# Gate products by row halves, interleaved score products and a wide head norm in a two-layer hybrid trunk

## The chip, the cores and the metric

The kernel runs on one core of a Trainium2 chip. The metric is the device time of one execution in microseconds; where a kernel was timed several times, the median stands. The trace is that of one profiled execution, whose own time is given beside its span. TensorE (PE in the rows) multiplies matrices, PEld is its loading of weights, VectorE is DVE, ScalarE is ACT, GpSimd is POOL, and SyncE (SP) issues the transfers of weights.

## What is computed

Two layers of a decoder trunk on 512 tokens with 1024 features, in float32. In each layer the RMS-normalised input goes through one wide projection; its columns feed three groups of token mixers, whose outputs, side by side, go through an output projection onto the residual. A convolutional feed-forward net follows. The parts that the change touches:

```python
def head_rmsnorm(o, w):
    y = o * rsqrt(mean(o * o, axis=-1) + NORM_EPS)        # per head of 64
    return y.reshape(B, S, H * d) * w

def rglru_group(xr, gr, ...):                             # 512 features in 8 blocks of 64
    xc = causal_dwconv(xr, conv_w, conv_b)
    r = sigmoid(block products of xc with wa + ba)        # 8 blocks, each 64 x 64
    i = sigmoid(block products of xc with wx + bx)
    log_a = -8 * r * softplus(-lam)
    u = sqrt(-expm1(2 * log_a)) * (i * xc)
    h = scan(h = exp(log_a) * h + u)
    return h * gelu(gr)

def retention_group(q, k, v, g, norm_w):                  # 4 heads of 64, chunks of 128
    per chunk: scores = (q k^T) * decay; o = scores v + (q state) * q_dec; state = ...
    return head_rmsnorm(o, norm_w) * silu(g)

x = x + concat(y_lru, y_ret, y_hg) @ w_out                # the output projection
```

The third mixer (HGRN2, 4 heads of 64) has a head norm of the same form.

## The kernel before

Features lie on the 128 partitions and the 512 tokens along the free axis, so a [128, 512] tile is two heads or two blocks of 64. Every large product takes both operands as two float32r parts (a rounded one, `h`, and the rest, `l`) and three matmuls of 512 columns: h·h, l·h and h·l (`mm3`, lines 320 to 322). The weights arrive as raw float32; for each weight tile ACT makes the rounded part (`wh`) and DVE the rest (`wl`), two tiles ahead of their use. In rows, `pps` is the input projection and the FFN's up projection, `vps` the values, `ops` the output projection, `dps` the FFN's down projection. The small products of the mixers go through `small` (line 326); most take plain float32 operands.

The order of every engine's instructions is written by a program, `Flow`. It emits the stream of large products, and keeps a rough clock of each engine; the mixers are chains (Python generators) whose next step is emitted when that clock says that the step before should be done. Engines then run their own instructions strictly in the emitted order, and wait for each other by data. So an instruction that is late holds up everything behind it on its engine, whatever it belongs to.

In a layer the chains run beside the input projection: first HGRN2 (`hg_...`), then retention in two pairs of heads (`rt_...`, `ft` = 0 and 1), and the RG-LRU (`lr_...`, four tiles `j`), first its four gate tiles, then in a batch twelve exponentials and hyperbolic tangents, four square roots and four scans. The batch waits for the head norms of HGRN2. Only one head norm of the wide kind (`head_norm`, `rsqrt_wide`) may run at a time (`hns`). At the end each of the eight mixed tiles is multiplied by its gate and split into `xh` and `xl` (`split_y`); a tile's place is free only when the last product of the input projection has read the old contents. The output projection reads the eight in the order `YORDER`: two of HGRN2, then the two retention pairs, then four of the RG-LRU. Its first two output tiles each take the first six inputs, then both take the last two.

What the change touches, before:

- RG-LRU gates: `lw` holds the blocks of both weights as block-diagonal 128 x 128 matrices. Per `j` there are two plain float32 products of 128 rows and 512 columns (`lr_ps`), one for each gate, and one sigmoid on 128 partitions for each.
- Retention scores: for each head four products of 64 rows with 128 x 128 results (`rt_ps`), the two heads of a pair one after the other, each with its own wait for a bank.
- Retention's head norm (`head_norm_cols`): squares, four narrow products that put token sums in columns (`hn_ps<-csm,sq`), an inverse root by bit trick and three Newton steps in a dozen small DVE operations (`hc_...`), and eight products that spread the result over the features again (`hn_rps`).
- `head_norm`, until now only HGRN2's: squares, their two float32r parts, two products with a matrix of means (`hn_ps<-hn_h`, `hn_ps<-hn_l`), then Ln, Exp and Square on ACT and three wide operations on DVE.

Of the kernel before, what the change touches and what calls it, by code (L numbers as in the profile page):

```python
# [7 lines left out]
F32 = mybir.dt.float32  # L8
# [33 lines left out]
# columns of the packed float constants  # L42
# [15 lines left out]
# W_in tiles in the order of use: (kind, column, contraction half)  # L58
# [10 lines left out]
# order in which the mixed features enter the output projection  # L69
# [84 lines left out]
class Timed:  # L154
    """An engine whose instructions are counted on the flow's clock."""
# [49 lines left out]
def kernel(ctx, tc, x_in, win, wout, wup, wdn, lruw, params, consts, out):  # L205
    nc = tc.nc

    const = ctx.enter_context(tc.tile_pool(name="const", bufs=1))
# [128 lines left out]
    def rsqrt_cols(pool, ps, shape, name, bufs=1):  # L337
        # seed from the exponent bits, then three Newton steps to full float32
        v = pool.tile(shape, F32, name=f"{name}_v", bufs=bufs)
        r = pool.tile(shape, F32, name=f"{name}_rc", bufs=bufs)  # L340
        t = pool.tile(shape, F32, name=f"{name}_nt", bufs=bufs)
        V.tensor_scalar(out=v, in0=ps, scalar1=EPS, scalar2=None, op0=ALU.add)
        V.tensor_scalar(out=r.bitcast(I32), in0=v.bitcast(I32), scalar1=1, scalar2=None,
                        op0=ALU.logical_shift_right)
        V.tensor_scalar(out=r.bitcast(I32), in0=r.bitcast(I32), scalar1=-1, scalar2=0x5F3759DF,
                        op0=ALU.mult, op1=ALU.add)
        for _ in range(3):
            V.tensor_tensor(out=t, in0=r, in1=r, op=ALU.mult)
# [65 lines left out]
    def finish_norm(n):  # L414
        if n.wide:
            # rb is -2 times the rstd
# [77 lines left out]
    def matmul_tiles(n, count, done, first=False, freed=None):  # L494
        """count weight tiles against the normed input; the first two of a phase leave its last parts for later."""
# [26 lines left out]
    def mixers(l, n):  # L522
# [31 lines left out]
        def head_norm(src, on, key):  # L554
            yield from hns.take()
            sq = mp.tile([128, S], F32, name="lr_a", bufs=4)
            v = mp.tile([128, S], F32, name="lr_a", bufs=4)
# [8 lines left out]
            drop(hns)  # L566
            on[key] = src
# [98 lines left out]
        # -- HGRN2 --  # L666
# [114 lines left out]
        # -- RG-LRU --  # L781
        lw = mp.tile([128, 2, 4, 128], F32, name="lw")
        nc.sync.dma_start(out=lw, in_=lruw[l])

        xc2, xcs, hst = {}, {}, {}

        def lru_conv(j):
# [13 lines left out]
            xcs[j] = xc  # L801
            evt.add(("xc", j))

        def lru_batch():
            js = range(4)
            gts, av = {}, {}
            for j in js:
                yield has(("xc", j))
                pss = []
                for w in range(2):  # L810
                    pss.append((yield from psum([128, S], "lr_ps")))
                for w in range(2):
                    small(0.857, out=pss[w], lhsT=lw[:, w, j, :], rhs=xcs[j])
                yield None
                gts[j] = []
                for w, bn in ((0, "lba"), (1, "lbx")):
                    g = mp.tile([128, S], F32, name=f"lr_g{w}", bufs=4)
                    A.activation(out=g, in_=pss[w], func=AF.Sigmoid, bias=pc(l, bn, j))
                    drop(sm)
                    gts[j].append(g)  # L820
# [41 lines left out]
        # -- retention --  # L862
# [24 lines left out]
        def ret_chain(ft):  # L887
# [6 lines left out]
            st = mp.tile([128, 2, NC, 128], F32, name="st", bufs=2)  # L894
            for h in range(2):
                hd = 2 * ft + h
                hs = slice(64 * h, 64 * h + 64)
                ps = yield from psum([128, NC, 128], "rt_ps")
                for c in range(NC):
                    cs = slice(c * 128, (c + 1) * 128)  # L900
                    small(0.11, out=ps[:, c, :], lhsT=rk[hs, cs], rhs=rq[hs, cs])
                yield None
                V.scalar_tensor_tensor(out=st[:, h], in0=ps, scalar=kin[:, hd:hd + 1],
# [20 lines left out]
            yield from head_norm_cols(o, ron, ("r", ft))  # L924
# [5 lines left out]
        for j in range(4):  # L930
            fl.spawn(lru_conv(j))
            fl.spawn(lru_gate(j))
        fl.spawn(lru_batch())
# [48 lines left out]
        # output projection, added to the residual  # L982
# [39 lines left out]
    def ffn(l, n, nxt):  # L1022
# [69 lines left out]
        def down_and_norm(gi):  # L1092
            # last group by halves of the tokens: the final norm of one half runs beside the other
# [103 lines left out]
    def main():  # L1197
        # the table of the activations is loaded while the first transfers run
# [4 lines left out]
        # the first tiles: input, first weights and constants in the order of need  # L1203
# [68 lines left out]
def _layout(inputs):  # L1272
# [34 lines left out]
    lruw = np.zeros((DEPTH, 128, 2, 4, 128), a["lru_wa"].dtype)  # L1307
    for i, nm in enumerate(("lru_wa", "lru_wx")):
        for b in range(8):
            o = 64 * (b % 2)  # L1310
            lruw[:, o:o + 64, i, b // 2, o:o + 64] = a[nm][:, b]
    ps = []
    for l in range(DEPTH):
        ps += [
            cols(a["norm1_w"][l]), cols(a["norm2_w"][l]), cols(a["lru_conv_w"][l].reshape(-1)),
            cols(a["lru_conv_b"][l]), cols(a["lru_ba"][l]), cols(a["lru_bx"][l]), cols(a["lru_lambda"][l]),
# [65 lines left out]
```

## Time and profile before

| | |
|---|---|
| median of 3 runs | 1201.98 us (1201.81 to 1202.22) |
| span of the profiled execution | 1199.86 us; about 2.1 us of the time lie around the span |
| TensorE | 1176.6 us busy, 98% of the span |
| VectorE, ScalarE, GpSimd | 812.2, 512.6 and 100.7 us busy |
| chain that ended last | TensorE 92% of the span, VectorE 5% |
| mean granted clock of TensorE | 0.995 of full speed |

A matmul's duration in the rows overlaps its neighbours, so the distance between the starts of two products is what one costs the stream. Plain float32 products leave two records each (k_o, rt_ps, lr_ps, hn_ps<-csm and hg_pl), the transposes and the float32r products one; an `x8` is then four products. In the pieces of the chain the duration is the time until the next instruction goes on.

### The profile page before, as it was taken

To read this page: it belongs to the slowest core of one execution; us is meant where nothing else is said; L and a number is where in the kernel's file an instruction comes from. 1 tells how busy PE (TensorE), PEld (TensorE's weight loads), DVE (VectorE), ACT (ScalarE), POOL (GpSimd) and SP (SyncE) were. 2 spreads that over 40 slices of the span, in tenths; PEclk is the share of its full clock that TensorE was granted. 3 is DMA by queue.
4 is the path that set the end of the run, shared out by engine and by line. 5 is a ranking of instruction groups with operands and counts; after the bars stand their busy time and mean duration, and the time that the engine had idled before them with its cause. 6 is when DMAs were issued, how large, how long until landed. Compare 5 with 4: busy or idle time off the path is not lost.

```text
span 1199.9 us, 15340 instructions
## 1 busy us (share of the span) xinstructions
PE 1176.6 (98%) x6044; PEld 967.0 (81%) x6044; DVE 812.2 (68%) x1218; ACT 512.6 (43%) x689; POOL 100.7 (8%) x85
## 2 busy tenths in 40 slices
PE   7989989999999999999999999999999999999996
PEld 6877778888888888888887877788888888888886
DVE  6797878558675467375579775865876746655746
ACT  5414684454443244142441445644544423423423
POOL 0131240000000000000223211400000000000001
PEclk9999999999999999999999999999999999999998
DMA  7222213232323332322341221222223232233221
GB/s 252 86 72 63 78 54 106 88 105 89 104 81 95 108 99 79 119 83 76 108 138 62 63 88 54 87 106 94 100 88 106 67 116 100 88 103 104 79 80 75
DMA packets 36312, 112.29 MB, mean 94 GB/s; under 512 B 4496, under 2 KB 4752, under 8 KB 36240
## 3 DMA queue, kind: packets, MB, share of 16 engines
q1 hardware_dynamic: 34704, 109.22, 28.4%
q10 hardware_dynamic: 1536, 2.10, 0.7%
q8 instruction: 47, 0.77, 0.3%
q14 instruction: 25, 0.20, 0.1%
HBM read 107.10 MB, written 2.10 MB: 91 GB/s over the span
## 4 chain that ended last, share of the span: by engine, by line
PE 92%; DVE 5%; issue 1%; DMA 0%; POOL 0%; SPq 0%; ACT 0%; POOLq 0%; DVEq 0%; ACTq 0%
PE pps L320 19%; PE pps L322 19%; PE pps L321 19%; PE dps L322 7%; PE dps L320 7%; PE dps L321 7%; PE ops L322 2%; PE ops L320 2%; PE ops L321 2%; DVE qp L181 1%; DVE st L181 1%; PE k_o L326 1%; PE lr_ps L326 1%; PE vps L320 1%; PE vps L322 1%
## 5 line engine op out<-in xcount | busy, mean ns | idle before, releaser
L320 PE MATMUL pps<-xh,wh 128*128 128x512 f32 x1024 | 410.1, 400 | 6.8 <-ACT wh L181 5.5
L322 PE MATMUL pps<-xh,wl 128*128 128x512 f32 x1024 | 401.8, 392 | 0.5 <-DVE wl L181 0.5
L321 PE MATMUL pps<-xl,wh 128*128 128x512 f32 x1024 | 401.7, 392 | 0.0
L181 ACT ACTIVATE wh<-raw 128x1024 fp32r<-128x1024 f32 (+2 forms) x210 | 204.4, 976 | 156.1 <-PE dps L321 103.3
L181 DVE TENSOR_TENSOR wl<-raw,wh 128x1024 fp32r<-128x1024 f32 (+2 forms) x210 | 242.1, 1156 | 18.9 <-ACT wh L181 18.8
L320 PEld LDWEIGHTS pps<-xh,wh 128*128 128x128 f32 x1024 | 193.4, 189 | 51.7 <-ACT wh L181 5.5
L322 PEld LDWEIGHTS pps<-xh,wl 128*128 128x128 f32 x1024 | 193.3, 189 | 42.9 <-DVE wl L181 1.2
L321 PEld LDWEIGHTS pps<-xl,wh 128*128 128x128 f32 x1024 | 193.6, 189 | 41.4 <-issue 1.7
L181 DVE SCALAR_TENSOR_TENSOR hs<-pps,rb 128x512 f32<-128x512 f32 x88 | 60.4, 690 | 128.8 <-PE pps L322 128.7
L322 PE MATMUL dps<-gh,wl 128*128 128x512 f32 x320 | 124.5, 389 | 0.0
L320 PE MATMUL dps<-gh,wh 128*128 128x512 f32 x320 | 124.5, 389 | 0.0
L321 PE MATMUL dps<-gl,wh 128*128 128x512 f32 x320 | 124.5, 389 | 0.0
L181 DVE TENSOR_TENSOR x<-x,dps 128x512 f32<-128x512 f32 (+1 forms) x72 | 45.1, 627 | 107.3 <-PE dps L322 106.8
L181 ACT ACTIVATE cg<-hs,prm 128x512 f32<-128x512 f32 x44 | 36.0, 817 | 81.2 <-DVE hs L181 76.6
L320 PEld LDWEIGHTS dps<-gh,wh 128*128 128x128 f32 x320 | 60.1, 188 | 12.5
L321 PEld LDWEIGHTS dps<-gl,wh 128*128 128x128 f32 x320 | 60.1, 188 | 12.5
L322 PEld LDWEIGHTS dps<-gh,wl 128*128 128x128 f32 x320 | 60.1, 188 | 12.4
L181 DVE SCALAR_TENSOR_TENSOR cvv<-hs,prm,cvv 128x511 f32<-128x511 f32 x88 | 65.8, 748 | 1.8
L181 DVE SCALAR_TENSOR_TENSOR cg<-hs,prm,cg 128x511 f32<-128x511 f32 x88 | 65.7, 747 | 1.5
L181 ACT ACTIVATE cg<-cg 128x512 f32<-128x512 f32 x44 | 27.8, 632 | 87.2 <-DVE cg L181 87.1
L181 ACT ACTIVATE gh<-cvv 128x512 fp32r<-128x512 f32 x44 | 27.7, 631 | 76.6 <-DVE cvv L181 76.6
L320 PE MATMUL ops<-xh,wh 128*128 128x512 f32 x128 | 50.5, 395 | 0.0
(207 smaller groups left out, 1330.8 us busy)
## 6 DMA issues: line engine op xcount, KB each, us to landing
raw<-in_wup_dram SPq DMA_DIRECT2D x88, 512.0 KB, 3.5
raw<-in_win_dram SPq DMA_DIRECT2D x46, 512.0 KB, 3.5
raw<-in_wdn_dram SPq DMA_DIRECT2D x48, 384.0 KB, 3.0
raw<-in_wout_dram SPq DMA_DIRECT2D x16, 512.0 KB, 3.6
raw<-in_wdn_dram SPq DMA_DIRECT2D x16, 256.0 KB, 2.6
x<-in_x_dram SPq DMA_DIRECT2D x8, 256.0 KB, 5.5
sw<-ev ACTq DMA_DIRECT2D x32, 64.0 KB, 2.1
out_dram<-hs SPq DMA_DIRECT2D x7, 256.0 KB, 2.0
```

The lines of the kernel that those rows point to most:

```text
L181: return fn(*args, **kw)
L320: T.matmul(out=ps, lhsT=ah, rhs=bh, start=start, stop=False)
L321: T.matmul(out=ps, lhsT=ah, rhs=bl, start=False, stop=False)
L322: T.matmul(out=ps, lhsT=al, rhs=bh, start=False, stop=stop)
L326: T.matmul(**kw)
```

## The change

- RG-LRU gates: `lw` is packed anew: the 64 rows of a block carry its columns for both gates side by side. ACT and DVE split it into `lwh` and `lwl` once a layer, and each convolved tile into `xch` and `xcl`. Per `j` there are six float32r products of 64 rows, 128 results and 512 columns, in turn on the upper and the lower half of the rows, into two banks; then four sigmoids on 64 partitions.
- Retention scores: both banks are taken first, and the eight products of a pair alternate between the heads, that is between the row halves.
- Retention's head norm: `head_norm` with `late=True`, in turn with HGRN2's on the one slot; `head_norm_cols` is not called any more.
- A pool `low` holds the new tiles; `dynamic_dma_scratch_size=1024` is set when the program is built. Lines of comment are gone.

```diff
-        def head_norm(src, on, key):
+        def head_norm(src, on, key, late=False):
             yield from hns.take()
-            sq = mp.tile([128, S], F32, name="lr_a", bufs=4)
-            v = mp.tile([128, S], F32, name="lr_a", bufs=4)
+            if late:
+                yield from sqs.take()
+                sq = mp.tile([128, S], F32, name="sq", bufs=2)
+                v = low.tile([128, S], F32, name="rn_v")
+            else:
+                sq = mp.tile([128, S], F32, name="lr_a", bufs=4)
+                v = mp.tile([128, S], F32, name="lr_a", bufs=4)
...
+        def lru_weights():
+            yield has(("hg_done", 0))
+            A.activation(out=lwh, in_=lw, func=AF.Copy)
+            yield None
+            V.tensor_tensor(out=lwl, in0=lw, in1=lwh.bitcast(F32), op=ALU.subtract)
...
+            h = low.tile([128, S], F32R, name="xch", bufs=2)
+            lo = low.tile([128, S], F32R, name="xcl", bufs=2)
+            A.activation(out=h, in_=xc, func=AF.Copy)
+            yield None
+            V.tensor_tensor(out=lo, in0=xc, in1=h.bitcast(F32), op=ALU.subtract)
...
-                for w in range(2):
-                    small(0.857, out=pss[w], lhsT=lw[:, w, j, :], rhs=xcs[j])
+                h, lo = xcp[j]
+                for p, (w, v) in enumerate(((lwh, h), (lwh, lo), (lwl, h))):
+                    for b in range(2):
+                        bs = slice(64 * b, 64 * b + 64)
+                        small(0.12, out=pss[b], lhsT=w[bs, j, :], rhs=v[bs, :], start=p == 0, stop=p == 2)
                 yield None
-                gts[j] = []
-                for w, bn in ((0, "lba"), (1, "lbx")):
-                    g = mp.tile([128, S], F32, name=f"lr_g{w}", bufs=4)
-                    A.activation(out=g, in_=pss[w], func=AF.Sigmoid, bias=pc(l, bn, j))
+                gts[j] = [mp.tile([128, S], F32, name=f"lr_g{w}", bufs=4) for w in range(2)]
+                for b in range(2):
+                    for w, bn in ((0, "lba"), (1, "lbx")):
+                        to = slice(64 * b, 64 * b + 64)
+                        at = slice(64 * (b ^ w), 64 * (b ^ w) + 64)
+                        A.activation(out=gts[j][w][to, :], in_=pss[b][at, :], func=AF.Sigmoid,
+                                     bias=pc(l, bn, j)[at, :])
...
+            pss = []
+            for h in range(2):
+                pss.append((yield from psum([128, NC, 128], "rt_ps")))
+            for c in range(NC):
+                cs = slice(c * 128, (c + 1) * 128)
+                for h in range(2):
+                    hs = slice(64 * h, 64 * h + 64)
+                    small(0.12, out=pss[h][:, c, :], lhsT=rk[hs, cs], rhs=rq[hs, cs])
...
-            yield from head_norm_cols(o, ron, ("r", ft))
+            yield from head_norm(o, ron, ("r", ft), late=True)
```

Since the order is made by the planner's clock, it moves in many places. Three of them follow. First TensorE in layer 0, at the first output tile (`ops`). Before, the products of the first and the second retention pair (`xh_1838`, then `xh_1846`) stand side by side:

```order
L320 MATMUL ops<-xh_1838,wh 128x512
L321 MATMUL ops<-xl_1839,wh 128x512
L322 MATMUL ops<-xh_1838,wl 128x512
L320 MATMUL ops<-xh_1846,wh 128x512
L321 MATMUL ops<-xl_1847,wh 128x512
L322 MATMUL ops<-xh_1846,wl 128x512
```

After, `xh_1898` is the first retention pair and `xh_1919` the second; the sums of squares for the second pair's norm stand between them:

```order
L321 MATMUL ops<-xh_1898,wh 128x512
L322 MATMUL ops<-xl_1899,wh 128x512
L323 MATMUL ops<-xh_1898,wl 128x512
L327 MATMUL hn_ps<-hn_h,hmean 128x512
L327 MATMUL hn_ps<-hn_l,hmean 128x512
L321 MATMUL ops<-xh_1919,wh 128x512
L322 MATMUL ops<-xl_1920,wh 128x512
L323 MATMUL ops<-xh_1919,wl 128x512
```

The last head norm has moved from some 90 products ahead of the output projection into it.

Second, ACT in layer 0 behind the twelve exponentials of the RG-LRU batch. Before (`qp` are the four square roots, `sq<-ev` sigmoids of gates, `ev<-ev` the GeLU):

```order
L181 ACTIVATE wh<-raw 128x1024 x2
L181 ACT_TABLE_LOAD
L181 ACTIVATE qp<-qp 128x512 x4
L181 ACT_TABLE_LOAD
L181 ACTIVATE sq<-ev 128x512 x2
L181 ACTIVATE wh<-raw 128x1024
L181 ACT_TABLE_LOAD
L181 ACTIVATE ev<-ev 128x512
L181 ACTIVATE wh<-raw 128x1024
```

After, with the Ln and the Exp of the first retention pair's norm (`rn_v`):

```order
L181 ACT_TABLE_LOAD
L181 ACTIVATE rn_v<-hn_ps,eps 128x512
L181 ACTIVATE wh<-raw 128x1024 x2
L181 ACT_TABLE_LOAD
L181 ACTIVATE qp<-qp 128x512 x4
L181 ACT_TABLE_LOAD
L181 ACTIVATE sq<-ev 128x512
L181 ACT_TABLE_LOAD
L181 ACTIVATE rn_v<-rn_v 128x512
L181 ACT_TABLE_LOAD
L181 ACTIVATE ev<-ev 128x512 x2
```

The norm's steps stand between those of the batch, each with a table of its own.

Third, DVE in layer 1 ahead of the output projection. Before (`lr_g<-lr_a,qp` is a scan, `rt_on` a retention pair, `xl` the last part of a mixed tile):

```order
L181 TENSOR_TENSOR ev<-pps,rb 128x512
L181 TENSOR_TENSOR wl<-raw,wh 128x1024
L181 TENSOR_TENSOR xl_6356<-hg_on,xh_6355 128x512
L181 TENSOR_TENSOR xl_6362<-hg_on,xh_6361 128x512
L181 TENSOR_TENSOR xl_6372<-rt_on,xh_6371 128x512
L181 TENSOR_TENSOR lr_g_6033<-lr_g_6033,ev 128x512
L181 TENSOR_TENSOR xl_6379<-rt_on,xh_6378 128x512
```

After:

```order
L181 TENSOR_TENSOR xl_6370<-hg_on,xh_6369 128x512
L181 TENSOR_TENSOR xl_6377<-hg_on,xh_6376 128x512
L181 SCALAR_TENSOR_TENSOR rt_on<-rt_on,prm,ev 128x512
L181 TENSOR_TENSOR xl_6387<-rt_on,xh_6386 128x512
L181 TENSOR_TENSOR lr_g_6137<-lr_g_6137,ev 128x512
L181 TENSOR_TENSOR wl<-raw,wh 128x1024 x2
L181 TENSOR_TENSOR xl_6424<-lr_g_5918,xh_6423 128x512
L181 TENSOR_TENSOR xl_6431<-lr_g_6021,xh_6430 128x512
L181 TENSOR_TENSOR lr_g_6159<-lr_g_6159,ev 128x512
L181 TENSOR_TENSOR xl_6452<-rt_on,xh_6451 128x512
```

The second retention pair's `xl` has moved from two places behind the first pair's to seven places behind it, with its multiplication by the gate just ahead of the first pair's `xl`.

## Rows read from the trace of the kernel before

**Rows 1.** The page: span, and TensorE's busy time with its share and instructions.
```profile
span 1199.9 us, 15340 instructions
PE 1176.6 (98%) x6044; PEld 967.0 (81%) x6044; DVE 812.2 (68%) x1218; ACT 512.6 (43%) x689; POOL 100.7 (8%) x85
```

**Rows 2.** Waits of TensorE: line, waited for, us in total, times, longest.
```profile
PE hn_rps L326 <- DVE hc_rc L181: 3.2, 1, 3.2
```

**Rows 3.** A stretch after that wait: length, busy time by engine, granted clock 0.51, DMA.
```profile
180.30:183.60 3.30, 3.30 (x12) 2.52 (x9) 3.30 (x5) 1.58 (x2) 0.00 (x0) 0.51 0.52 158
```

**Rows 4.** Chain that ended last, small products: start, us until the next, instruction.
```profile
82.84 0.61 PE hg_pl L326 x16
...
97.55 1.08 PE rt_ps L326 x8
...
109.62 3.65 PE k_o L326 x56
...
118.36 0.79 PE hn_ps L326 x8
122.03 1.72 PE lr_ps L326 x4
125.83 1.02 PE hn_rps L326 x16
...
135.73 0.47 PE hn_ps L326 x2
...
153.75 0.50 PE k_mps L326 x12
...
156.54 1.83 PE k_o L326 x28
...
688.53 1.83 PE k_o L326 x28
```

**Rows 5.** Timeline of TensorE in layer 0: start, duration, instruction, count.
```profile
95.66 0.87 PE L326 MATMUL k_o<-qp,k_sv 64*64 64x128 f32 x12
96.46 1.09 PE L326 MATMUL hg_pl<-qp,k 128*64 128x128 f32 x8
```

**Rows 6.** Timeline of TensorE, output projection of layers 0 and 1, first and fourth input.
```profile
197.36 0.40 PE L320 MATMUL ops<-xh,wh 128*128 128x512 f32 x1
...
199.46 0.39 PE L320 MATMUL ops<-xh,wh 128*128 128x512 f32 x1
...
783.65 0.39 PE L320 MATMUL ops<-xh,wh 128*128 128x512 f32 x1
```

**Rows 7.** Timeline of ACT in layer 0: table load, exponentials, weights, four square roots.
```profile
152.45 1.28 ACT L181 ACT_TABLE_LOAD   x1
153.74 0.72 ACT L181 ACTIVATE lr_a<-lr_g,lamc 128x512 f32<-128x512 f32 x1
...
161.69 1.04 ACT L181 ACTIVATE wh<-raw 128x1024 fp32r<-128x1024 f32 x1
...
168.41 2.19 ACT L181 ACTIVATE qp<-qp 128x512 f32<-128x512 f32 x4
```

**Rows 8.** ACT's gate sigmoids, both layers: busy, mean ns of one, idle before.
```profile
L181 ACT ACTIVATE lr_g<-lr_ps,prm 128x512 f32<-128x512 f32 x16 | 10.8, 687 | 16.3 <-PE lr_ps L326 16.3
```

**Rows 9.** Timeline of DVE in layer 1: scan, weights, and 512-column operations.
```profile
774.12 1.21 DVE L181 TENSOR_TENSOR_SCAN lr_g<-lr_a,qp 128x512 f32<-128x512 f32 x1
775.26 1.19 DVE L181 TENSOR_TENSOR wl<-raw,wh 128x1024 fp32r<-128x1024 f32 x1
...
777.04 0.68 DVE L181 TENSOR_TENSOR lr_g<-lr_g,ev 128x512 f32<-128x512 f32 x1
777.64 0.68 DVE L181 TENSOR_TENSOR ev<-pps,rb 128x512 f32<-128x512 f32 x1
```

**Rows 10.** Timeline of POOL in layer 1: the four products ahead of the scans.
```profile
758.96 7.91 POOL L181 TENSOR_TENSOR qp<-qp,lr_g 128x512 f32<-128x512 f32 x4 [1.09 <-ACT qp L181]
```

More of the change, by code (lines that the diff above doesn't have):

```diff
@@ L206 @@
     nc = tc.nc
+    low = ctx.enter_context(tc.tile_pool(name="low", bufs=1, reuse_waits="tile"))
     const = ctx.enter_context(tc.tile_pool(name="const", bufs=1))
@@ L566, in head_norm @@
             drop(hns)
+            if late:
+                drop(sqs)
             on[key] = src
@@ L779, in hg_chain @@
             yield from head_norm(o, hon, ("h", ft))
-        lw = mp.tile([128, 2, 4, 128], F32, name="lw")
+        lw = mp.tile([128, 4, 128], F32, name="lw")
         nc.sync.dma_start(out=lw, in_=lruw[l])
-        xc2, xcs, hst = {}, {}, {}
+        lwh = low.tile([128, 4, 128], F32R, name="lwh")
+        lwl = low.tile([128, 4, 128], F32R, name="lwl")
+        xc2, xcs, hst, xcp = {}, {}, {}, {}
+        def lru_weights():
[4 more added lines that the diff above has]
+            yield None
+            evt.add("lw")
         def lru_conv(j):
@@ L801, in lru_conv @@
             xcs[j] = xc
+            h = low.tile([128, S], F32R, name="xch", bufs=2)
+            lo = low.tile([128, S], F32R, name="xcl", bufs=2)
+            A.activation(out=h, in_=xc, func=AF.Copy)
+            yield None
+            V.tensor_tensor(out=lo, in0=xc, in1=h.bitcast(F32), op=ALU.subtract)
+            yield None
+            xcp[j] = h, lo
             evt.add(("xc", j))
@@ L808, in lru_batch @@
                 yield has(("xc", j))
+                yield has("lw")
                 pss = []
-                for w in range(2):
+                for b in range(2):
                     pss.append((yield from psum([128, S], "lr_ps")))
-                for w in range(2):
-                    small(0.857, out=pss[w], lhsT=lw[:, w, j, :], rhs=xcs[j])
-                yield None
-                gts[j] = []
-                for w, bn in ((0, "lba"), (1, "lbx")):
-                    g = mp.tile([128, S], F32, name=f"lr_g{w}", bufs=4)
-                    A.activation(out=g, in_=pss[w], func=AF.Sigmoid, bias=pc(l, bn, j))
+                h, lo = xcp[j]
[3 more added lines that the diff above has]
+                        small(0.12, out=pss[b], lhsT=w[bs, j, :], rhs=v[bs, :], start=p == 0, stop=p == 2)
+                yield None
+                gts[j] = [mp.tile([128, S], F32, name=f"lr_g{w}", bufs=4) for w in range(2)]
+                for b in range(2):
+                    for w, bn in ((0, "lba"), (1, "lbx")):
[3 more added lines that the diff above has]
+                                     bias=pc(l, bn, j)[at, :])
                     drop(sm)
-                    gts[j].append(g)
                 G.tensor_tensor(out=gts[j][1], in0=gts[j][1], in1=xcs[j], op=ALU.mult)
@@ L894, in ret_chain @@
             st = mp.tile([128, 2, NC, 128], F32, name="st", bufs=2)
+            pss = []
[6 more added lines that the diff above has]
+                    small(0.12, out=pss[h][:, c, :], lhsT=rk[hs, cs], rhs=rq[hs, cs])
+            yield None
             for h in range(2):
                 hd = 2 * ft + h
[L897 to L903, printed above, removed]
+                V.scalar_tensor_tensor(out=st[:, h], in0=pss[h], scalar=kin[:, hd:hd + 1],
                                        in1=tri.unsqueeze(1).to_broadcast([128, NC, 128]), op0=ALU.mult, op1=ALU.mult)
@@ L932, in mixers @@
             fl.spawn(lru_gate(j))
+        fl.spawn(lru_weights())
         fl.spawn(lru_batch())
@@ L1306, in _layout @@
     wdn = np.stack(wdn)
-    lruw = np.zeros((DEPTH, 128, 2, 4, 128), a["lru_wa"].dtype)
+    lruw = np.zeros((DEPTH, 128, 4, 128), a["lru_wa"].dtype)
     for i, nm in enumerate(("lru_wa", "lru_wx")):
         for b in range(8):
-            o = 64 * (b % 2)
-            lruw[:, o:o + 64, i, b // 2, o:o + 64] = a[nm][:, b]
+            o, to = 64 * (b % 2), 64 * (b % 2 ^ i)
+            lruw[:, o:o + 64, b // 2, to:to + 64] = a[nm][:, b]
     ps = []
@@ L1315, in _layout @@
             cols(a["norm1_w"][l]), cols(a["norm2_w"][l]), cols(a["lru_conv_w"][l].reshape(-1)),
-            cols(a["lru_conv_b"][l]), cols(a["lru_ba"][l]), cols(a["lru_bx"][l]), cols(a["lru_lambda"][l]),
+            cols(a["lru_conv_b"][l]), cols(a["lru_ba"][l]), np.roll(cols(a["lru_bx"][l]), 64, axis=0), cols(a["lru_lambda"][l]),
             cols(a["ret_norm_w"][l]), cols(a["hg_norm_w"][l]), cols(a["hg_lower_bounds"][l]),
@@ L1368 @@
     from concourse.bass_utils import run_bass_kernel_spmd
-    nc = bacc.Bacc("TRN2", target_bir_lowering=False, num_devices=1)
+    nc = bacc.Bacc("TRN2", target_bir_lowering=False, num_devices=1, dynamic_dma_scratch_size=1024)
     arrays, args = {}, []
```

## The prediction

> **What bounds the kernel now.** I read the page first: TensorE is busy for 1176.6 of 1199.9 us [rows 1]. Then its waits: inside the mixers only one is longer than 1 us, 3.2 us ahead of a head norm's spreading products in layer 0, where it waits for the small DVE operations of the Newton steps [rows 2]; the 3.3 us after it run at a granted clock of 0.51, the lower of the two levels, 1.2 GHz [rows 3]. Half of that, 1.6 us, is lost. So time saved on TensorE is time saved, as long as the other engines deliver by then. That second half decides here, so I read next how closely ACT, DVE and POOL run ahead of the output projection, in both layers [rows 6 to 10], and followed the new order with those durations.
>
> **TensorE's own saving.** One large product costs the stream (199.46 - 197.36) / 9 = 0.233 us [rows 6].
>
> Gates: a tile's two plain products cost 1.72 us [rows 4], eight tiles in both layers. Six float32r products come instead. If the two row halves run at once, that is 3 x 0.233 = 0.70 us, with the return to full rows 0.85; if not, 6 x 0.233 + 0.15 = 1.55. The rows show no product that uses row halves alone, in turn. The nearest: the score products, on one row half each, take 1.08 / 8 = 0.135 us a record [rows 4], and the products with the states, of the same length and in turn on opposite quarters (64 rows and 64 columns), 0.80 us between their starts and the next, for 12 records: 0.067 [rows 5]. They are twice as fast, so I take 0.85 and a saving of 0.87 per tile, 7.0 us in all, with the other end kept as a rival.
>
> Scores: two groups of 1.08 us per pair of heads become one of 1.08 if the halves run at once: 4 x 1.08 = 4.3 us.
> Here a page speaks against the change. The Trainium skill (TensorE: Matmul & The Clock Gate, "LDWEIGHTS (loading the stationary operand)") lets a load take columns / 1.2 ns however few rows it has: 107 ns for 128 columns, 53 for 64. If the loads of both halves queued, sixteen records would take 1.71 us and the scores' saving would fall by 2.5 us. The trace has sixteen records with 64 columns in 0.61 us, 0.038 each [rows 4], below that page's 53 ns, so loads into two column halves do overlap; for row halves no row says it.
>
> Head norm: narrow squares 0.79 and spreading 1.02 go, two float32r products of 0.47 together come [rows 4]: 1.34 x 4 = 5.4 us. The wait of 3.2 us and its slow clock, 1.6, go too. Together 21.5 us, if nothing else became late.
>
> **What ACT and DVE get in return.** Four sigmoids for two per tile (they cost by columns, 0.69 each [rows 8]), the splits of eight tiles, and for each of four head norms a copy, Ln, Exp, Square and their tables. The program has 42 table loads for 33. A load costs from 152.45 to the next start at 153.74, 1.29 us [rows 7]. The small DVE operations of the Newton steps go, some ten 512-column ones (0.60 between two starts [rows 9]) come. None of this is a bound by itself: what counts is when the second retention pair, fourth input of the output projection, is there. Queued behind it on TensorE stands everything else of the layer.
>
> **Layer 0, step by step.** The state products of the first pair end at 109.62 + 3.65 = 113.3 [rows 4]; the scores ahead of them are one group shorter, so 112.2. By the new order, 147 large products follow until the fourth gate tile is done (34.3 us), the four gate tiles (3.4), one norm (0.47), the second pair's scores (1.08) and three transposes (about 0.3, an estimate from k_mps' 0.50 [rows 4]): 151.7, and with the returns to full rows 152.
> ACT then has that tile's four sigmoids (2.75), a weight tile (1.04 [rows 7]), two 512-column copies (0.55 each, a quarter of 2.19 [rows 7]) and a load: the exponentials start at 158.2, where they started at 153.74 before. They take 161.69 - 153.74 = 7.95 [rows 7]: 166.1. From there to the Square of the first retention norm the order has six weight tiles (6.2), six loads (7.7), four roots (2.2) and nine 512-column operations (5.0): 187.2.
> DVE is later still. The first root is done at 174.7; POOL's four products at 7.91 / 4 each [rows 10] end at 182.6, the last scan at 183.8 (1.21 [rows 9]). Then six 512-column operations and three weight parts of 1.14 (775.26 - 774.12 [rows 9]) until the norm's own: 190.8. Eight more, with the parts of the RG-LRU tiles among them, finish the first pair at 195.6, four more give the second norm's squares at 198.0. Their sums on TensorE 0.47, Ln, load, Exp, Square 2.9, four dependent DVE operations of 0.68, a copy: 204.7. No row times a change of engine by itself; for six of them I add 0.8: **205.5**.
> TensorE would be at that place at 152 + 0.5 + 1.83 + 0.47 + 129 x 0.233 = 184.9. So it waits some 20 us, in two pieces, and restarts slowly. Before, it passed there at 199.46 [rows 6]. With 1.6 us of slow clock: 205.5 + 1.6 - 199.5 = **+7.6 us**. Eight table loads lie on this path.
> At the loads a page and a row differ. The Trainium skill (ScalarE: Activation LUTs, "What ACT_TABLE_LOAD costs") adds a drain of some 1380 ns to each load of 1283. By that the eight loads would make the layer 11 us later and the time 1221. In the trace the next activation starts 1.29 us after the load does [rows 7], so no drain is seen and the sum stays.
>
> **Layer 1.** Here the norms come earlier and their Ln and Exp are covered. From the end of the state products, 688.53 + 1.83 = 690.4 [rows 4], less 1.08 and with three products more ahead (0.7): 690.0. Then 180 products (41.9), two norms, four gate tiles, the scores, transposes and states (8.1), returns (0.8): the last norm's sums at 740.8, the last but one projection tile at 766.4, the output projection at 772.0. But DVE takes its result from that tile and has then, in its order, fourteen 512-column operations, four scans and three weight parts ahead of and with the second pair's last part: 8.4 + 4.6 + 3.4 = 16.4, so 782.8. That product ran at 783.65 + 0.23 = 783.9 before [rows 6]. So 9 us of saving become a wait for DVE: -1.1, plus 1.6 for the clock: **+0.5 us**. DVE operations beside POOL can be slower; 2 us more are possible, 2 less if the scans are early.
>
> **Sum.** 1199.9 + 7.6 + 0.5 = 1208.0 of span, with the 2.1 around it 1210.1; the median lies where the profiled execution does. Feed-forward nets, the start and the end stay as they are. The smaller scratch and the new pool touch no queue that the rows show busy: nothing.
>
> **Rivals.**
> *The halves don't run at once.* Then every gate tile costs 0.7 more and each pair's scores 1.08, in both layers ahead of the late stretch: 4 x 0.7 + 2 x 1.08 = 5.0 per layer, as ACT waits for the fourth gate tile and DVE for the last tiles: 1220. For it: no row with row halves. Against it: rows 5.
> *Faster: the mixed tiles are in time.* If the second pair is ready when TensorE gets there, by 185 in layer 0 and 774 in layer 1, the whole 21.5 stays: 1180; it is faster from the point at which the pair comes more than 8 us earlier than I sum, at 197. It would need ACT's list of 29 us after the exponentials' start to be done beside something else. Against it: ACT works strictly in order, and these durations are back to back in the rows.
> *No change.* The stretch in layer 0 is some 6 us shorter than my sum of about fifty durations, mostly because DVE's last operations don't queue as I put them: 1200 to 1204.
>
> **How the numbers follow.** What a measurement of this kernel can tell from no change is about 0.2%, 2.4 us. The forecast, 1210 with 1204 to 1217 about it, has 0.60; halves in sequence 0.15; no change 0.12; faster 0.13. Faster 0.13, the same 0.12, slower 0.75. The range takes in all but the faster case and what lies above the sequential one: 1200 to 1222.
>
> **What would show it.** In the profile after: TensorE idle some 20 us between 183 and 206, released by the second pair's `xh` and `xl` of ACT and DVE, and some 8 us around 775 to 785 in layer 1; a granted clock of half after each; `lr_ps` groups of 0.85 us and score groups of 1.1 for eight products. I am wrong if the gate groups take 1.5, if the output projection of layer 0 starts without a wait, or if TensorE waits for weights instead.

## The result and the profile after

The changed kernel takes 1219.39 us (median; 1218.79 to 1219.70) against 1202.10 us of the kernel before in the same session: 17.3 us more, ratio 1.014 with an interval of 1.0128 to 1.0152. The direction and the whole range of the forecast (1200 to 1222) held; its size did not, +8.1 us was forecast, and the time lies above the 1204 to 1217 given about the forecast itself.

The page of the profiled execution after, its span and TensorE's busy time, answers [rows 1]; the third line is the granted clock of TensorE in 40 equal slices, in tenths.

```profile
span 1217.9 us, 15224 instructions
...
PE 1169.2 (96%) x5972; PEld 960.4 (79%) x5972; DVE 811.0 (67%) x1192; ACT 550.6 (45%) x740; POOL 102.2 (8%) x85
...
PEclk9999995999999999999999999979999999999998
```

TensorE has 7.4 us less work by the records and yet the span is 18.0 us longer. Two slices have a low clock, the seventh and the 27th: the output projections of the two layers. TensorE's waits (line, waited for, us in total, times, longest) say the same; the wait of [rows 2] is gone, and 29.5 us stand in its place:

```profile
PE ops L322 <- DVE xl L181: 14.8, 4, 7.0
PE ops L321 <- ACT xh L181: 14.7, 3, 7.1
```

In the timeline of TensorE (start, duration, instruction, and in brackets the idle time before with what ended it) these are, first in layer 0 and then in layer 1, the longest of them:

```profile
190.28 0.80 PE L322 MATMUL ops<-xl,wh 128*128 128x512 f32 x1 [4.49 <-DVE xl L181]
...
198.94 0.80 PE L321 MATMUL ops<-xh,wh 128*128 128x512 f32 x1 [6.15 <-ACT xh L181]
...
209.23 0.80 PE L321 MATMUL ops<-xh,wh 128*128 128x512 f32 x1 [7.08 <-ACT xh L181]
...
792.49 0.79 PE L322 MATMUL ops<-xl,wh 128*128 128x512 f32 x1 [7.00 <-DVE xl L181]
...
799.63 0.80 PE L322 MATMUL ops<-xl,wh 128*128 128x512 f32 x1 [2.94 <-DVE xl L181]
```

The row at 190.28 waits for HGRN2's tiles and the one at 198.94 for the first retention pair; the row at 209.23 is the second pair's first product, the place that [rows 6] has at 199.46 before. In layer 1 the longer wait, at 792.49, is for HGRN2's tiles too, and the one at 799.63 for the second pair. After each of the two last waits TensorE runs at the lower of its two levels, 1.2 GHz; windows of TensorE (length, busy time and instructions, granted clock, DMA):

```profile
209.20:213.90 4.70, 4.67 (x10) 0.50 0.00 0
799.60:804.50 4.90, 4.87 (x12) 0.50 0.18 71
```

The lower level begins earlier in both layers, while TensorE is still waiting for tiles; these are its whole stretches:

```profile
186.75:214.05 27.30, 10.19 (x21) 0.50 0.17 58
787.49:804.56 17.07, 9.13 (x21) 0.50 0.29 92
```

So 19.3 us of the busy time in the records were spent at the lower clock, which is why they show only 7.4 us less although more work than that was taken off TensorE.

The small products that the change made are as short as forecast. In the chain that ended last (start, us until the next, instruction): a norm's sums, a gate tile, the scores of one pair.

```profile
132.21 0.47 PE hn_ps L327 x2
...
134.05 0.90 PE lr_ps L327 x6
...
140.71 1.09 PE rt_ps L327 x16
```

A gate tile's six products take 0.90 us where two took 1.72 [rows 4], and the scores of two heads 1.09 where one head's took 1.08.

To see in which layer the time lies I use one tile, `rms_ps`: its first kind of product belongs to the norm ahead of a layer's mixers, its second to the norm ahead of a layer's feed-forward net. The rows give the first and the last start of each kind, so layer 0's mixers take 252.9 - 24.2 = 228.7 us before and 265.1 - 24.1 = 241.0 after, layer 1's 225.3 and 231.3. Before, and then after:

```profile
L326 PE MATMUL rms_ps<-csm,ssq x16: 164/250/250, 24.2 to 612.0; 128*128 128x1 f32 x16
L326 PE MATMUL rms_ps<-sq,ones x4: 391/392/392, 252.9 to 837.3; 128*128 128x512 f32 x4
```

```profile
L327 PE MATMUL rms_ps<-csm,ssq x16: 164/250/251, 24.1 to 624.3; 128*128 128x1 f32 x16
L327 PE MATMUL rms_ps<-sq,ones x4: 391/392/392, 265.1 to 855.6; 128*128 128x512 f32 x4
```

So layer 0 lost 12.3 us (7.6 forecast) and layer 1 lost 6.0 (0.5 forecast).

### The profile page after: what moved, and what is told of

It is laid out like the page before. It is cut to its first block, busy times and chain, and to the rows that moved or that the text cites. A ratio compares the mean times of both kernels' runs of the same rounds, so it can differ in the third digit from the quotient of the medians.

```text
span 1217.9 us, 15224 instructions
## 1 busy us (share of the span) xinstructions
PE 1169.2 (96%) x5972; PEld 960.4 (79%) x5972; DVE 811.0 (67%) x1192; ACT 550.6 (45%) x740; POOL 102.2 (8%) x85
## 4 chain that ended last, share of the span: by engine, by line
PE 85%; DVE 10%; ACT 2%; issue 2%; DMA 0%; POOL 0%; SPq 0%; POOLq 0%; DVEq 0%
PE pps L321 18%; PE pps L322 17%; PE pps L323 17%; PE dps L321 7%; PE dps L322 7%; PE dps L323 7%; PE ops L322 3%; PE ops L323 2%; PE ops L321 2%; DVE st L181 2%; DVE wl L181 2%; DVE qp L181 2%; DVE lr_g L181 1%; PE k_o L327 1%; PE vps L321 1%
## 5 line engine op out<-in xcount | busy, mean ns | idle before, releaser
L322 PE MATMUL ops<-xl,wh 128*128 128x512 f32 x128 | 54.5, 426 | 14.8 <-DVE xl L181 14.8
L321 PE MATMUL ops<-xh,wh 128*128 128x512 f32 x128 | 53.8, 421 | 14.7 <-ACT xh L181 14.7
```

Of the source, the lines that this page charges most:

```text
L321: T.matmul(out=ps, lhsT=ah, rhs=bh, start=start, stop=False)
L322: T.matmul(out=ps, lhsT=ah, rhs=bl, start=False, stop=False)
```

## The experiments

Medians, ratio to the kernel before with its interval, and the change of each layer's mixers against the kernel before, taken from the rows of `rms_ps` in each run's profile as above:

| run | us | ratio | layer 0 | layer 1 |
|---|---|---|---|---|
| the change | 1219.39 | 1.0128 to 1.0152 | +12.3 | +6.0 |
| e1_narrow_norm | 1205.81 | 1.0023 to 1.0045 | +5.1 | -0.5 |
| e2_norm_alone | 1220.22 | 1.0131 to 1.0161 | +10.6 | +8.3 |
| e3_products_on_dve | 1215.99 | 1.0092 to 1.0122 | +9.9 | +5.2 |
| e4_retention_read_last | 1214.96 | 1.0086 to 1.0116 | +8.5 | +4.4 |
| e5_before_products_on_dve | 1197.16 | 0.9949 to 0.9973 | -4.6 | -0.1 |
| e6_before_dve_and_scores | 1193.22 | 0.9917 to 0.9941 | -7.1 | -1.4 |
| e7_norm_without_tables | 1217.45 | 1.0118 to 1.0144 | +10.7 | +5.3 |
| e8_halves_one_after_other | 1221.85 | 1.0146 to 1.0177 | +13.4 | +6.0 |
| e9_no_products | 1214.54 | 1.0085 to 1.0116 | +10.3 | +2.7 |
| e10_second_norm_narrow | 1209.16 | 1.0051 to 1.0079 | +9.8 | -2.6 |
| e11_narrow_norm_dve | 1206.11 | 1.0026 to 1.0054 | +3.6 | +2.0 |
| e12_first_norm_wide | 1202.49 | 1.0000 to 1.0018 | +3.7 | -4.6 |
| e13_two_sigmoids | 1205.47 | 1.0022 to 1.0044 | +2.3 | +2.0 |
| e14_first_norm_wide_layer1 | 1189.99 | 0.9892 to 0.9923 | -6.9 | -4.7 |

### Which part of the change costs

e1 takes the wide norm out of the change, e2 puts it alone into the kernel before:

```
-            yield from head_norm(o, ron, ("r", ft), late=True)
+            yield from head_norm_cols(o, ron, ("r", ft))
```

> The changed kernel with retention's head norm put back to the narrow products; the split gates and the scores in turn stay. Theory A (the late second retention pair, and with it the wide norm's chain on ACT and DVE, is what costs the time; the gates and scores only bring TensorE a saving that the other engines take up): TensorE keeps 11 us of saving, ACT and DVE are about where they were, and the time is 1196 to 1205. Rival B (the gates' four sigmoids and the splits make everything late, the norm is harmless): 1212 or more. Rival C (the norm is the only loss, the saving of gates and scores stays whole): 1202 - 11 = 1191.

> The kernel before with only the wide retention norm; gates and scores as before. Theory A: the second norm has its Ln, Exp, Square and their table loads behind the RG-LRU work on ACT and its DVE steps behind the scans, so the output projection of layer 0 waits for the second pair: 1208 to 1216. Rival B (norm harmless): TensorE's 10 us are saved, 1190 to 1196.

The norm alone costs 18.1 us and the other two parts alone 3.7; together they cost 17.3. So the norm is the loss, and rival B is out in both runs; theory A of e2 has the direction, but the time lies 4.2 us above its range. With the norm in, gates and scores bring TensorE's saving of some 11 us nowhere. e1 lies 0.8 us above the upper end of theory A: gates and scores are not neutral but a small loss.

e10 keeps the wide norm for the first pair alone (`if ft: head_norm_cols`, else `head_norm`).

> The changed kernel with the wide norm for the first retention pair alone, the narrow products for the second. Theory A (the second pair's wide norm, last in every queue, is what costs): nearly all of the loss of the norm goes, 1204 to 1209. Rival L (each of the two norms costs about half, by its table loads on ACT and its place in DVE's queue): 1211 to 1214.

1209.16, 0.2 above theory A's upper end: 10.2 of the 13.6 us that the norm adds to e1 belong to the second pair. What is left of it is split by layer: against e1 the first pair's wide norm costs 4.7 us in layer 0 and gains 2.1 in layer 1.

### POOL beside DVE

In the prediction the scans have 1.21 us each, from [rows 9]. After, DVE's timeline in layer 0 has 8.79 us for four, in layer 1 5.60 for three, and neighbours are long too; POOL's products run beside them:

```profile
177.32 8.79 DVE L181 TENSOR_TENSOR_SCAN lr_g<-lr_a,qp 128x512 f32<-128x512 f32 x4 [1.70 <-POOL qp L181]
...
778.26 2.31 DVE L181 TENSOR_TENSOR wl<-raw,wh 128x1024 fp32r<-128x1024 f32 x1
780.49 0.68 DVE L181 TENSOR_TENSOR ev<-pps,rb 128x512 f32<-128x512 f32 x1
781.09 1.18 DVE L181 SCALAR_TENSOR_TENSOR rt_on<-rt_on,rn_v 128x512 f32<-128x512 f32 x1
782.20 5.60 DVE L181 TENSOR_TENSOR_SCAN lr_g<-lr_a,qp 128x512 f32<-128x512 f32 x3
```

```profile
752.93 1.29 POOL L181 TENSOR_TENSOR lr_g<-lr_g,qp 128x512 f32<-128x512 f32 x1 [5.87 <-ACT lr_g L181]
...
175.99 6.89 POOL L181 TENSOR_TENSOR qp<-qp,lr_g 128x512 f32<-128x512 f32 x4 [4.61 <-ACT qp L181]
182.85 2.19 POOL L181 TENSOR_TENSOR ev<-ev,sq 128x512 f32<-128x512 f32 x1
...
776.40 7.03 POOL L181 TENSOR_TENSOR qp<-qp,lr_g 128x512 f32<-128x512 f32 x4 [4.08 <-ACT qp L181]
```

Both sides pay: a POOL product takes 1.29 us while DVE is idle (the row at 752.93), 1.72 to 1.76 on the mean of four here, and 2.19 beside the last scan of layer 0. The operation that reads `pps` from PSUM keeps its 0.68 us in the same stretch. Three runs test it. e3 moves the four products of each layer to DVE, in the changed kernel; e9 leaves them out; e5 does e3's edit to the kernel before:

```
-                G.tensor_tensor(out=xcs[j], in0=xcs[j], in1=gts[j][1], op=ALU.mult)
+                V.tensor_tensor(out=xcs[j], in0=xcs[j], in1=gts[j][1], op=ALU.mult)
```

> The changed kernel with the four products ahead of the scans of each layer on DVE instead of POOL. Theory D (DVE operations stretch while POOL works: the scans of layer 0 take 2.2 us each beside POOL's products and 1.2 without): four products cost DVE 2.4 us per layer, the scans shrink by 4 us in layer 0, in layer 1 scans and neighbours by 4: the scans of layer 0 end 3 us earlier, and the time is 1213 to 1216. Rival E (the scans are slow by themselves, for where their operands lie): they stay at 2.2 us and the four products come on top, 1222 to 1225.

> The changed kernel with the four products ahead of the scans of each layer left out (the scans read the roots themselves; the planner still counts the products, so that DVE and ACT keep their order). Theory D (POOL's products stretch what DVE does beside them): the scans of layer 0 take 1.2 us each instead of 2.2 and begin 1.5 us earlier, DVE's stretch of layer 1 is 4.7 us shorter, and the time falls by 7 to 10 us: 1209 to 1212. Rival E (the scans are long by themselves): they stay at 2.2 us and only the wait for the first product goes, 1217 to 1218.

> The kernel before with the four products ahead of the scans of each layer on DVE instead of POOL, nothing else. Theory D (DVE stretches beside POOL; in the kernel before five of the small Newton operations of layer 0 take 1.1 to 1.2 us beside POOL's products, 0.17 without): these shrink by some 5 us, the wait of 3.2 us ahead of the spreading products and its 1.6 us of half clock go: 1196 to 1199. Rival E (no stretching by POOL, the products are a plain addition of 2.4 us to a DVE that delivers just in time): 1203 to 1206.

e3 and e5 fall where theory D put them, 1215.99 and 1197.16; e5 is faster than the kernel before by 4.4 us, although DVE got four operations more per layer. In e9 the scans are short, so theory D holds and E is out, but the time, 1214.54, is 2.5 us above its range. The timeline of DVE in e9 shows where that went:

```profile
177.76 4.57 DVE L181 TENSOR_TENSOR_SCAN lr_g<-lr_a,qp 128x512 f32<-128x512 f32 x4 [0.28 <-ACT qp L181]
185.15 1.29 DVE L181 TENSOR_TENSOR lr_g<-lr_g,ev 128x512 f32<-128x512 f32 x2 [2.83 <-ACT ev L181]
```

With the scans done early, DVE waits 2.8 us for ACT's gates: ACT, with its table loads, is the next bound in layer 0, and takes back part of what DVE gained in layer 0 (layer 0 gains 2.0 us by e9, layer 1 3.3).

The kernel before had the effect already, at the very wait that the prediction named as TensorE's only long one [rows 2]. The small operations of the Newton steps in DVE's timeline, then POOL's products, both before:

```profile
171.81 0.15 DVE L181 TENSOR_SCALAR hc_v<-hn_ps 128x8 f32<-128x8 f32 x1
172.00 1.07 DVE L181 TENSOR_SCALAR hc_rc<-hc_v 128x8 int32<-128x8 int32 x1
173.10 1.22 DVE L181 TENSOR_SCALAR hc_rc<-hc_rc 128x8 int32<-128x8 int32 x1
174.36 1.20 DVE L181 TENSOR_TENSOR hc_nt<-hc_rc 128x8 f32<-128x8 f32 x1
...
178.06 0.17 DVE L181 TENSOR_TENSOR hc_nt<-hc_rc 128x8 f32<-128x8 f32 x1
```

```profile
169.18 6.36 POOL L181 TENSOR_TENSOR qp<-qp,lr_g 128x512 f32<-128x512 f32 x4 [2.74 <-ACT qp L181]
175.50 2.50 POOL L181 TENSOR_TENSOR ev<-ev,sq 128x512 f32<-128x512 f32 x2
```

Eight columns take 0.17 us without POOL and 1.07 to 1.22 beside it, until POOL is done at 178.0. Only the operation that reads PSUM, `hc_v`, is short. In e5, where POOL has no more than the two gating products there, two of these operations are long instead of five, and the wait of [rows 2] is gone.

The Trainium skill (SBUF — State Buffer, "Who interferes with whom") has the rule: VectorE and GpSimd share one pair of SBUF ports, a VectorE instruction with two SBUF inputs contends with a GpSimd instruction that reads SBUF, and that pair is an exclusive lock. The rows with two SBUF inputs agree: beside POOL a scan and the small operation at 174.36 both become about 1 us longer (1.14 to 2.2, 0.17 to 1.20), which is most of one POOL product and no fixed factor, and the operations that read PSUM are spared. The two small `TENSOR_SCALAR` rows at 172.00 and 173.10 have one SBUF input and stretch all the same; the sentence on two inputs does not reach them.

### What else lies on the late path

e4 lets the output projection read the RG-LRU tiles ahead of the retention pairs:

```
-YORDER = [6, 7, 4, 5, 0, 1, 2, 3]
+YORDER = [6, 7, 0, 1, 2, 3, 4, 5]
```

> The changed kernel with the output projection reading the RG-LRU tiles before the retention pairs. Theory A: in layer 0 some 24 products more run before TensorE needs the second pair, at half the clock in part; the pair itself comes some 2 us later, since its norm's sums queue behind them: 4 to 5 us less in layer 0, little in layer 1, where DVE delivers all tiles within a few us: 1213 to 1217. Rival F (the RG-LRU tiles are as late as the pair): within 1 us of 1219.

1214.96, inside theory A's range: 3.8 us less in layer 0 and 1.6 in layer 1. TensorE then waits for several tiles' `xl`, 16.9 us in six waits in all: 11.5 for HGRN2's, as in the change, and 5.4 for the RG-LRU's. The pair is the last of several late tiles.

e7 takes the table loads out (in `rsqrt_wide`, for retention alone, `AF.Ln` and `AF.Exp` become `AF.Identity` with small scales).

> The changed kernel with Ln and Exp of retention's wide norm replaced by a plain scaling (the norm's values are left out by this), so that the order of all instructions stays and eight table loads go, four per layer. Theory G (a load costs 1.29 us where it lies on the path, and three of the four per layer lie beside other waits): the scans of layer 0 start 1.3 us earlier, the second norm is 1.3 us shorter, layer 1 gains 1.3: 1214 to 1217. Rival H (a load costs more, with a drain ahead of it): all eight times 2.7 us or most of it, below 1210. Rival I (the loads are hidden): 1219.

1217.45, 1.9 us less, 0.5 above theory G's range and far from H: of eight loads, 10.3 us of ACT's time, most lie beside other waits. The prediction set the row's 1.29 us against the drain that the Trainium skill (ScalarE: Activation LUTs, "What ACT_TABLE_LOAD costs") adds; by that the eight would be 21 us of ACT's time. A run in which most loads are hidden cannot tell the two lengths apart; it only shows that nothing of the larger size lies on the path. The length itself is read from the rows: the next activation starts 1.29 us after the load [rows 7], and in e11's rows below the load at 167.88 follows the activation ahead of it (167.23, 0.64 us) without a gap, too.

e8 puts a tile's six gate products half by half:

```
-                for p, (w, v) in enumerate(((lwh, h), (lwh, lo), (lwl, h))):
-                    for b in range(2):
-                        bs = slice(64 * b, 64 * b + 64)
+                for b in range(2):
+                    bs = slice(64 * b, 64 * b + 64)
+                    for p, (w, v) in enumerate(((lwh, h), (lwh, lo), (lwl, h))):
```

> The changed kernel with the gates' six products ordered by half: three on rows 0 to 63, then three on rows 64 to 127. Theory J (products on the two row halves run side by side only if they stand in turn): a gate group takes 1.5 us instead of 0.9, the exponentials of layer 0 start some 2 us later, and the time is 1221 to 1224. Rival K (the queue lets the halves overlap in any order): groups of 0.9 us and 1219.

The median, 1221.85, lies in theory J's range, but the trace refutes J. The chain of e8:

```profile
136.05 0.90 PE lr_ps L327 x6
147.12 0.90 PE lr_ps L327 x6
```

0.90 us as in the change, so rival K holds: the halves overlap in either order. The 2 us are there before any gate tile: the first such group starts 2.0 us later than in the change (127.54 against 125.54), with nothing altered ahead of it, and the single runs go from 1218.63 to 1222.26. I take e8 as no difference.

### Why gates and scores don't pay, and what does

e6 has, on the kernel before, the products on DVE and the scores in turn; e11 is e6 with the split gates.

> As the run before it, with the scores of two heads in turn as well. If DVE, relieved, delivers the mixed tiles in time, TensorE's 4.3 us of saving shows in full: about 4 us below the run before it, 1192 to 1195. If DVE and ACT set when the output projection starts, most of it becomes a wait there: within 1 us of the run before it.

> Split gates and scores in turn, narrow norm, and the products ahead of the scans on DVE: the sixth run with the split gates added. Theory A (the gates' four sigmoids for two and the splits of the conv tiles take more from ACT and DVE than the 7 us that TensorE saves): 1198 to 1203, above the sixth run's 1193. Rival C (with DVE relieved the gates' saving shows): 1186 to 1189.

e6 shows nearly all of the scores' saving, 3.9 of 4.3 us below e5: with DVE relieved, the mixed tiles are in time. e11 misses both theories: at 1206.11 the split gates cost 12.9 us where TensorE saves 7, and relieving DVE brought nothing against e1. In its profile the exponentials of the RG-LRU in layer 0 start at 169.2 us; in the kernel before at 153.74 [rows 7], in e6 at 152.3. ACT's timeline in e11, just ahead of them:

```profile
159.61 2.77 ACT L181 ACTIVATE lr_g<-lr_ps,prm 64x512 f32<-64x512 f32 x4 [2.04 <-PE lr_ps L327]
...
162.94 1.04 ACT L181 ACTIVATE wh<-raw 128x1024 fp32r<-128x1024 f32 x1
167.23 0.64 ACT L181 ACTIVATE sq<-ev 128x512 f32<-128x512 f32 x1 [3.24 <-DVE ev L181]
167.88 1.28 ACT L181 ACT_TABLE_LOAD   x1
169.18 0.72 ACT L181 ACTIVATE lr_a<-lr_g,lamc 128x512 f32<-128x512 f32 x1
```

The last gate sigmoid is done at 162.4, but a gating sigmoid that needs a projection tile not yet computed stands ahead of the exponentials in ACT's queue. That is the smaller part of the delay. In e6 the last gate sigmoid is done at 149.4, so 13.0 of the 16.9 us are there before. ACT waits for TensorE at that point, and TensorE's fourth gate tile, in e6 and then in e11, is late by its place:

```profile
146.83 1.88 PE L326 MATMUL lr_ps<-qp,lw 128*128 128x512 f32 x4
```

```profile
158.61 0.50 PE L327 MATMUL lr_ps<-xch,lwh 64*128 64x512 f32 x2
```

In TensorE's rows 564 products of the input projection and the values stand ahead of it in e11, 516 in e6; 48 at 0.233 us are 11.2. e13 asks whether the number of sigmoids matters, with two of 128 rows for four of 64:

```
-                for b in range(2):
-                    for w, bn in ((0, "lba"), (1, "lbx")):
...
+                for w, bn in ((0, "lba"), (1, "lbx")):
+                    A.activation(out=gts[j][w], in_=pss[w], func=AF.Sigmoid, bias=pc(l, bn, j))
```

> The eleventh run (split gates, scores in turn, narrow norm, products on DVE) with two sigmoids of 128 rows per gate tile instead of four of 64 (the swap of halves between the two gates is left out by this; the planner still counts four, so the order stays). Theory M (the four sigmoids, 1.4 us more of ACT per tile, are what makes the split gates dear): some 4 to 6 us per layer less work ahead of the exponentials, 1197 to 1201. Rival N (the place of the exponentials in ACT's queue is: ACT waits 3.2 us for a projection tile ahead of them in layer 0, so that shorter sigmoids only lengthen the wait): 1204 to 1206.5.

1205.47, in rival N's range. In e13 the wait ahead of the same gating sigmoid is 3.61 us instead of 3.24, and that ahead of the fourth tile's gate sigmoids is twice as long:

```profile
156.01 1.27 ACT L181 ACTIVATE lr_g<-lr_ps,prm 128x512 f32<-128x512 f32 x2 [4.12 <-PE lr_ps L327]
```

Most of what ACT saves it waits for TensorE. So the work of the four sigmoids, with the order kept, is 0.6 of the 12.9 us. That the place of the gate tiles in TensorE's order, and behind it that of the exponentials in ACT's, makes most of the rest is argued from these rows; which step of the new chains (the splits, or the four sigmoids as the planner counts them) moved that place was not tried, so this stays open.

Last, whether the wide norm is bad in itself. e12 gives e6 the wide norm for the first pair in both layers, e14 in layer 1 alone.

> The sixth run (kernel before, products on DVE, scores in turn) with the wide norm for the first retention pair alone. If its chain is early enough to be covered: TensorE's 1.34 us per layer show, 1190 to 1191.5. If its table loads and DVE steps delay the RG-LRU work: 1194 to 1200.

> The sixth run (kernel before, products on DVE, scores in turn) with the wide norm for the first retention pair of layer 1 alone. In the twelfth run layer 1, between the sums of its two input norms, took 3.2 us less than in the sixth, layer 0 10.8 us more. If a layer's gain is its own: 1189 to 1191. If layer 1 was short there only for what layer 0 had left it: 1193 to 1196.

e12 fits neither of its theories: 10.8 us more than e6 in layer 0 and 3.2 less in layer 1. So the gain and the loss are each a layer's own, and e14, 1189.99, keeps the gain alone: 0.8 to 1.1% faster than the kernel before, the lowest median of all, though its interval and e6's overlap at the edge. The loss in layer 0 is not a late start of the exponentials, which in e12 begin at 147.0, 5.3 us earlier than in e6. TensorE's longest wait there is ahead of the second pair's narrow norm, at 196.46:

```profile
PE hn_rps L327 <- DVE hc_rc L181: 4.7, 1, 4.7
```

So with the first pair's norm wide the second pair's comes late: ACT makes its squares at 187.90, in e6 at 162.21. The two kinds of `rms_ps` products in e14, and its first waits:

```profile
L327 PE MATMUL rms_ps<-csm,ssq x16: 164/250/250, 24.5 to 605.4; 128*128 128x1 f32 x16
L327 PE MATMUL rms_ps<-sq,ones x4: 391/392/392, 246.3 to 826.0; 128*128 128x512 f32 x4
```

```profile
PE pps L321 <- ACT wh L181: 6.0, 1, 6.0
PE hg_pl L327 <- DVE hg_p L181: 3.6, 3, 2.0
```

None of the waits in the mixers' last stretch is left, neither for a norm nor for a mixed tile. Of the gain in layer 1, 1.34 us are TensorE's by the forecast's rows; 1.4 more are a wait of e6 that e14 does not have:

```profile
PE pps L322 <- DVE wl L181: 1.4, 1, 1.4
```

## Why the prediction was right or wrong

**TensorE's terms were right.** 0.90 us per gate tile (0.85 forecast), 1.09 per pair of scores, 0.47 per norm, and the wait of 3.2 us gone. Of the two readings that stood side by side the row's held: the sixteen records of a pair's eight score products in 1.09 us are 0.068 us each, below the 107 ns per load of 128 columns that the Trainium skill (TensorE: Matmul & The Clock Gate, "LDWEIGHTS (loading the stationary operand)") gives. Each record has its own load, so here loads for the two row halves overlap too.

**The mechanism was right.** The saving turned into waits for the second retention pair in layer 0 and for DVE in layer 1, as forecast: in layer 0 five waits of together 19.5 us between 184 and 209 (some 20 between 183 and 206 forecast), with the lower clock behind the last. Only the last 7.1 of them are released by the second pair itself, where the forecast's signs put all on it; the others, for HGRN2's tiles and the first pair, come first, and the second pair's arrival sets when the layer goes on. The rival with halves one after the other gave 1220, almost the time measured, and is false all the same: only the groups of 0.90 us show that. A time that fits does not choose between mechanisms.

**The term that was mis-sized is DVE's work beside POOL**, in both layers. The step "the last scan at 183.8" took a scan's 1.21 us from a row of [rows 9] at which POOL was already done. Measured it ended at 186.1, 2.3 us later, and DVE came to the norm at 193.03 instead of 190.8. In e9, without POOL's products, four scans take 4.57 us, 1.14 each, so the forecast's duration is right where POOL is still. That e9 then comes to the norm at 192.17, which is 190.3 on the scale of the change (it was 1.85 us late ahead of the scans, 174.52 against 172.67) and so near the forecast, is chance: its scans end 3.3 us ahead of the forecast's, and then comes the wait of 2.83 us for ACT, which the forecast does not have. In layer 1 the step "8.4 + 4.6 + 3.4 = 16.4" had the same row: the three scans are 2.1 us longer, the other operations from 771.9 on together 2.4 (weight parts of 1.48 and 2.31 for 1.14, norm operations of 1.07 and 1.18 for 0.6 to 0.7). The second pair's product came at 799.63, which is 787.3 without layer 0's 12.3; 782.8 was forecast, 4.5 less. The prediction allowed 2 us for this, without a price for it. The hint was in its own rows: [rows 10] has 7.91 us for four POOL products, 1.98 each, where a lone one takes 1.29 (at 740.81 in the same trace). The two pieces, 2.3 and 4.5 us, are 6.8 of the 9.3 us by which the time exceeds the forecast; e9 got 4.9 back, for in layer 0 ACT is the next bound.

**Two smaller terms.** The lower clock costs half of 4.7 and of 4.9 us, 2.4 each, where 1.6 was taken from [rows 3]. And from the second norm's squares (198.0 forecast, the end of their last operation at 200.63 measured) to its pair took 8.6 us instead of 7.5; its two sums alone took 0.87 for 0.47, because TensorE was at the lower level by then. In the chain:

```profile
201.30 0.87 PE hn_ps L327 x2
```

Added up: 3.7 us at 209.23, 4.5 in layer 1 and 1.6 of clock make 9.8, against those 9.3.

## What to carry to other kernels

Take a duration from a row in which the other engines do what they will do after the change; here VectorE and GpSimd slow each other down, so a VectorE duration without its neighbour's timeline is half a number, and work given to an idle GpSimd can cost more than it relieves. A saving on the busiest engine counts only as far as the last operand it waits for comes earlier too: test the parts of a change one by one, since the part that saved least on paper (the scores) was the only one that paid as it stood, on the kernel with the products on DVE. And the place of a chain in its layer, not its length, decides: the same wide norm cost 10.8 us in one layer and gained 3.2 in the other.

## What was not expected of the hardware

- Small VectorE operations of 0.17 us between tiles in SBUF take 1.07 to 1.22 us while GpSimd works on tiles in SBUF, and GpSimd's 1.29 us become 1.7 to 2.0 on the mean of four, 2.19 in one case; operations that read PSUM keep their time (0.68 us).
- Products on the two row halves overlap whether they stand in turn or half by half: 0.90 us for six in both orders.
- After the last wait of each layer's stretch, 7.1 and 2.9 us, TensorE stayed at a granted clock of 0.50 for 4.7 and 4.9 us of large products without a gap; the 3.3 us of [rows 3] had been read as the usual length.
